# Row block 0's products with V's weights from float32 rows and weights, and the row norms' powers on GpSimd

## The chip, the cores and the metric

The kernel runs on one core of a Trainium2 chip. The core has five engines with instruction streams of their own, each worked off in order: TensorE (PE, matrix products; its weight loads are shown as PEld), VectorE (DVE), ScalarE (ACT), GpSimd (POOL) and SyncE (SP, which here issues the DMA transfers). They wait for one another by semaphores. The metric is the time of one execution on the device, in microseconds.

## The reference

One layer of an encoder for 1024 tokens of width 1024, all in float32:

```python
u = rms_norm(x, norm1_g[l])
proj = u @ w_in[l]
q, k, v, cb, cc, ch, ga, gb = jnp.split(proj, split_pts, axis=-1)
q = rms_norm(q.reshape(B, S, N_HEADS, HEAD_DIM), q_norm_g[l])
k = rms_norm(k.reshape(B, S, N_HEADS, HEAD_DIM), k_norm_g[l])
y_a = neighbourhood_attention(q, k, v, rpb[l]) @ w_attn_branch[l]
y_b = short_gated_conv(cb, cc, ch, conv_w[l]) @ w_conv_branch[l]
merged = jax.nn.sigmoid(ga) * y_a + jax.nn.sigmoid(gb) * y_b
x = x + merged @ w_o[l]
h = rms_norm(x, norm2_g[l]) @ w_mlp_in[l]
x = x + jnp.square(jax.nn.relu(h)) @ w_mlp_out[l]
```

`rms_norm(x, g)` multiplies each row of x by one over the root of its mean square, and each column by g. q and k are normed in the same way over the 64 numbers of each head. What matters here is the start: the norm of x, and its product with the 512 columns of `w_in` that give v.

## The kernel before

**Number format.** A float32 operand is scaled by a power of two (so that its largest value fits) and written as two float16 halves, hi and lo, with hi + lo the value. A product of two such operands takes three passes on TensorE: hi·hi, hi·lo and lo·hi (`PASSES`, line 447; `HH`, `HL`, `LH` name them, the left letter for the rows, the right one for the weights).

**Rows.** The 1024 tokens are 8 row blocks of 128. Block b is loaded to `xt[:, b]` (L366). `norm` (L430) is a generator with one step per `yield`: ScalarE squares the block and sums each row (L433); `rstd` (L402) turns the sum into one over the root, `ys`, with a root on ScalarE (L407) and five small VectorE operations around it (L406 ahead of the root; the reciprocal L409 and one correction step, L411, L102 and L415, behind it); the high half is x times that factor, by GpSimd (L437), for block 0 by ScalarE (L439); the low half is VectorE's (L441). `ln_step(b, n)` advances block b's generator by n steps; written out among the other work, these calls set the order on each engine.

The halves must be turned so that the columns of x lie on the partitions, in `UT`. For blocks 0 to 2 TensorE does this with eight 128 x 128 transposes per half (`turn_row`, L525), copied out of PSUM by ScalarE for the high half (L530) and VectorE for the low half (L532). For blocks 3 to 7 a DMA does it (`ln_turn`, L444), issued by SP.

**V's weights** come in two chunks `v0`, `v1` of 1024 x 256. Each needs its power of two first: for v0 the largest absolute value (`L594`), for v1 a sum of squares (`v1_square`, L623); a product with ones (`v_sum`, L541) brings the 128 partitions together, `v_scale` (L544 and what follows, to L547) makes the factor. `v_part` writes the high parts on ScalarE (L555) and the low parts on VectorE (L557), eight of each per chunk. The gain `norm1_g` is part of the factor of each row of the weights.

**Products.** `v_mms(b, j, ks, passes)` (L571) issues products of 256 columns for row block b and chunk j: 24 for each pair, for b from 0 to 2. `v_post` brings the sum out of PSUM as two halves of v (L579, L581). From block 3 on, `v_unit` does both chunks in 24 products of 512 columns (called through `unit`, L210). Then come 8 such units for Q and 8 for K (`tok_mms`, also L210), where `qk_vec` norms each head: ScalarE copies and squares (L736, L737), VectorE sums the squares of 8 heads (L740), `rstd` makes 8 factors a row, VectorE multiplies (L744, L747, L750), and two more operations make the halves (L754, L756).

**What else is queued there.** Chunks of weights are loaded to 5 buffers (`load_upto`, L234, on SP), in the order V, Q, K and so on; a buffer is free when its chunk's low parts are written. Q's weights are prepared by a generator, `prep`, stepped by `tick` among the products (squares L266, high parts L306, low parts L297). After V's part, `sforms` scales the row blocks of `xt` in place (L482), forms sums and differences of them on GpSimd (L486), and stores them.

**PSUM.** There are eight banks: three with tag "d", three "s", two "o". Transposes and sums use "o".

Of the kernel before, what the change touches and what calls it, by code (L numbers as in the profile page):

```python
# [18 lines left out]
D = 1024  # L19
# [33 lines left out]
def encoder_block(ctx: ExitStack, tc: tile.TileContext, x, weights, cols, gqk, rel, masks, out):  # L53
# [25 lines left out]
    sc = base.tile([128, 512], F32, name="sc")  # L79
    sci = sc.bitcast(I32)  # L80
    area = {"keep": [0, 0, 144], "prep": [144, 144, 240], "tmp": [240, 240, 512]}
# [289 lines left out]
    A.activation(sc[:, warm], sc[:, warm], AF.Sqrt)  # L371
# [16 lines left out]
    V.tensor_scalar(ident, idi, 0.0, None, op0=OP.is_equal)  # L388

# [27 lines left out]

    def pow2_half(ss, top, s, inv, more=0):
# [11 lines left out]
    def norm(xin, sq, u, y, pool):  # L430
# [4 lines left out]
        yield from rstd(ss, D, y, 9)  # L435
# [32 lines left out]
    ln = [norm(xt[:, b], sq, u16[:, b % 4], at(ys, b), b > 0) for b in range(8)]  # L468
# [52 lines left out]
    def turn_row(b, s):  # L521
# [5 lines left out]
        def copy():  # L527
            o, i = UT[:, s, :, b * 128:(b + 1) * 128], pt.rearrange("p (k t) -> p k t", k=8)
            if s == 0:
                A.activation(o, i, AF.Copy)  # L530
            else:
                V.tensor_copy(o, i)  # L532
# [42 lines left out]

    def v_post(b, j, s):
        hi, lo = (VT[:, b, w, 256 * j:256 * j + 256] for w in range(2))
        if s == 0:
            A.activation(hi, vps[b, j][:, :256], AF.Copy, scale=2.0 ** -20)  # L579
        else:  # L580
            V.scalar_tensor_tensor(lo, vps[b, j][:, :256], 2.0 ** -20, hi, op0=OP.mult, op1=OP.subtract)  # L581
# [10 lines left out]
    ln_step(0, 7)  # L592
    for k, n in (0, 4), (4, 2), (6, 2):
        V.tensor_reduce(sc[:, at(v0.rm, k, n)], v0.raw[k // 4][:, k % 4 * 256:(k % 4 + n) * 256].rearrange(  # L594
            "p (k w) -> p k w", k=n), axis=AX, op=OP.max, apply_absolute_value=True)
    turn_row(0, 0)()
# [4 lines left out]
    v_sum(v0, c)  # L601
    ln_step(1)
    v_scale(v0, 1e-30, pow2(v0.b, 14, v0.s, v0.inv, False, v0.more))
    ln_step(0)
    v_part(v0, 0, range(3))
    ln_step(1)
    v_part(v0, 0, range(3, 8))
    ln_step(1, 5)
    v_mms(0, 0, (0, 1), HH)
    turn_row(0, 1)()  # L610
    v_part(v0, 1, lower)
    v_mms(0, 0, range(2, 7), HH)
    copy = turn_row(1, 0)
    v_mms(0, 0, (7,), HH)
    copy()
    v_mms(0, 0, eight, LH)
    v_mms(0, 0, lower, HL)
    ln_step(2)
    ln_step(1)
    v_mms(1, 0, eight, HH)  # L620

    def v1_square(p):
        A.activation(v1.parts[:, 1, 1024 * p:1024 * p + 1024].bitcast(BF16), v1.raw[p], AF.Square,  # L623
                     accum_out=sc[:, at(v1.rm, p)])

    v_part(v0, 1, (4,))
# [3 lines left out]
    ln_step(3)  # L630
    v_part(v0, 1, (5,))
    ln_step(2, 5)
    turn_row(1, 1)()
    v_mms(0, 0, (4, 5), HL)
    v_mms(1, 0, range(6), HL)
    v_part(v0, 1, (6, 7))
    v_mms(1, 0, eight, LH)
    copy = turn_row(2, 0)
    V.tensor_reduce(sc[:, v1.a], sc[:, at(v1.rm, 0, 2)], axis=AX, op=OP.add)
    c = ones_col()  # L640
    V.tensor_tensor(c, sc[:, v1.a], sc[:, gm2], op=OP.mult)
    v_sum(v1, c)
    v_mms(0, 0, (6, 7), HL)
    v_mms(1, 0, (6, 7), HL)
    copy()
    v_scale(v1, 1e-36, pow2_half(v1.b, 14, v1.s, v1.inv, v1.more))
    v_part(v1, 0, lower)
    ln_step(2)
    v_mms(2, 0, eight, HH, HL)
    ln_step(3)  # L650
    v_part(v1, 0, (4, 5))
    v_part(v1, 1, (0, 1))
    copy = turn_row(2, 1)
    ln_step(3, 5)
    copy()
    v_part(v1, 0, (6, 7))
    for b in 0, 1:
        v_mms(b, 1, lower, HH, LH)
    v_mms(2, 0, eight, LH)
    v_mms(2, 1, lower, HH, LH)  # L660
# [3 lines left out]
    v_post(1, 0, 0)  # L664
    ln_step(3)
    ln_turn(u16[:, 3], 3, UT)
    push(cQ)
    ln_step(4)
    v_part(v1, 1, (4, 5))
    tick()  # L670
    ln_step(5)
    ln_step(4, 5)
    for b in range(3):
        v_mms(b, 1, upper, HH, LH)
# [6 lines left out]
    turned[0] = 5  # L681
    ln_step(5)
    tick()
    ln_step(6)
    v_post(1, 0, 1)
    v_post(2, 0, 1)
    ln_step(5, 5)
    tick()
    for ks in lower, (4, 5), (6, 7):
        for b in range(3):  # L690
            v_mms(b, 1, ks, HL)
# [4 lines left out]
    turned[0] = 6  # L696
    ln_step(7)
    for b in range(3):
        v_post(b, 1, 0)
        v_post(b, 1, 1)  # L700
    ln_step(6, 5)
    tick()
    ln_step(7)
    ln_step(6)
    ln_turn(u16[:, 2], 6, UT)
    turned[0] = 7
    ln_step(7, 5)
# [25 lines left out]
    def qk_vec(ps, inv, kind, res):  # L733
# [8 lines left out]
        yield from rstd(ss, HD, y, 12 if kind == "q" else 0)  # L742
# [1201 lines left out]
```

## Time and profile before

| | |
|---|---|
| median of 3 runs | 1207.05 us (1206.65 to 1208.08) |
| span of the profiled execution | 1205.3 us |
| TensorE busy | 1188.0 us, 99% |
| VectorE busy | 938.7 us, 78% |
| ScalarE busy | 759.8 us, 63% |
| GpSimd busy | 433.1 us, 36% |

How to read the lines below: in the timeline a line has start and duration in us, engine, line of the kernel, operation, what is written and read, shapes, and the count of merged instructions; in brackets stands for how long the engine had been idle, and what released it. Matmuls overlap, so that the pace of a group is best read from the starts of successive groups. In the table of groups the numbers behind the bar are busy time in us and mean duration in ns, then the idle time ahead of them. In the table of stages each engine has its busy time and count, and PEclk is the granted clock of TensorE. Of one line's instructions the three numbers are the shortest, median and longest in ns, and the start of the first and the last in us. Waits are: waiting engine and line, what it waited for, total us, how often, the longest.

### The profile page before, as it was taken

What the parts mean: (1) busy time and instruction counts of PE and PEld (TensorE: products, weight loads), DVE (VectorE), ACT (ScalarE), POOL (GpSimd) and SP (SyncE); (2) the same over time, 40 slices, a digit from 0 to 9 for tenths busy, and PEclk for the clock granted to TensorE, in tenths of its full rate; (3) what the DMA queues carried; (4) which work ended last, traced back from release to release, by engine and by line L of the source; (5) the groups of instructions that cost most, each with busy time, mean ns of one, the idle gap of its engine ahead of it and who ended that gap; (6) DMA issues with size and microseconds to landing.
All of it is one profiled execution on the core that took longest, in us unless ns stands there. A gap on an engine that the chain in (4) does not pass through costs nothing.

```text
span 1205.3 us, 17076 instructions
## 1 busy us (share of the span) xinstructions
PE 1188.0 (99%) x6294; PEld 573.8 (48%) x6294; DVE 938.7 (78%) x1759; ACT 759.8 (63%) x1183; POOL 433.1 (36%) x280
## 2 busy tenths in 40 slices
PE   6999999999999999999999999999999999999998
PEld 4444445555444444444467444444444444444444
DVE  7777988988368787877878655545548999999997
ACT  7766679867554545337779778678676744746440
POOL 1640011222311112001004465565567471553662
PEclk9999999999999999999999999999999999999999
DMA  7766657676542211224386545445465925334202
GB/s 264 151 213 141 140 119 130 133 146 123 103 123 65 67 56 53 70 93 187 57 155 183 182 159 192 149 139 193 145 247 201 352 97 217 129 138 194 105 35 105
DMA packets 171012, 173.36 MB, mean 144 GB/s; under 512 B 131504, under 2 KB 132016, under 8 KB 166832
## 3 DMA queue, kind: packets, MB, share of 16 engines
q1 hardware_dynamic: 170352, 168.07, 47.9%
q10 hardware_dynamic: 576, 4.19, 0.8%
q8 instruction: 49, 0.80, 0.3%
q14 instruction: 35, 0.29, 0.1%
HBM read 102.51 MB, written 37.75 MB: 116 GB/s over the span
## 4 chain that ended last, share of the span: by engine, by line
PE 73%; DVE 9%; ACT 1%; issue 1%; DMA 1%; DVEq 0%; ACTq 0%
PE ps_d L210 26%; PE ps_s L210 23%; PE ps_o L210 16%; PE ps_d L1039 6%; DVE w_s L1163 2%; PE ps_o L1016 1%; PE ps_s L959 1%; DVE sg L1279 1%; DVE P L999 1%; DMA u2T<-v 1%; DVE sz L973 1%; ACT w_s L1167 0%; DVE sc L317 0%; DVE m L1281 0%; ACT sg L1245 0%
## 5 line engine op out<-in xcount | busy, mean ns | idle before, releaser
L210 PEld LDWEIGHTS <-ops 128*128 128x128 f16 x1356 | 132.4, 98 | 157.3
L210 PEld LDWEIGHTS <-w 128*128 128x128 f16 x1368 | 132.8, 98 | 140.0 <-DMA u2T<-v 0.6
L1039 PE MATMUL ps_d<-uT,w_ws 128*128 128x512 f16 x528 | 123.7, 379 | 0.1
L210 PE MATMUL ps_d<-ops 128*128 128x512 f16 (+1 forms) x528 | 118.3, 374 | 0.0
L1765 ACT ACTIVATE ops<-hf,sc 128x2048 f16<-128x2048 f32 x26 | 52.0, 2000 | 97.9 <-PE ps_o L210 35.2
L210 PE MATMUL ps_s<-ops 128*128 128x512 f16 x492 | 112.9, 379 | 0.0
L1152 POOL TENSOR_TENSOR tsum<-raw 128x512 f32<-128x512 f32 x28 | 46.0, 1658 | 149.6 <-ACT raw L1138 141.6
L1345 POOL TENSOR_TENSOR as<-as 128x512 f32<-128x512 f32 x56 | 77.5, 1384 | 39.3 <-ACT as L1625 36.0
L210 PEld LDWEIGHTS <-w_s 128*128 128x128 f16 x588 | 56.8, 98 | 69.4 <-DVE w_s L1163 1.9
L210 PE MATMUL ps_d<-u2x,w 128*128 128x512 f16 (+1 forms) x360 | 80.0, 372 | 0.0
L210 PEld LDWEIGHTS <-uT 128*128 128x128 f16 x504 | 49.0, 98 | 59.6 <-DMA uT<-u 0.8
L1039 PEld LDWEIGHTS <-w_ws 128*128 128x128 f16 x528 | 51.2, 98 | 54.5 <-DVE cv L861 0.4
L210 PE MATMUL ps_o<-ops 128*128 128x512 f16 x336 | 77.1, 379 | 0.0
L1767 DVE SCALAR_TENSOR_TENSOR ops<-hf,sc,ops 128x2048 f16<-128x2048 f32 x26 | 74.0, 2846 | 3.7 <-ACT ops L1765 3.7
L210 PE MATMUL ps_o<-u2T,w 128*128 128x512 f16 (+1 forms) x324 | 71.7, 371 | 0.0
L1138 ACT ACTIVATE raw<-raw,sc 128x256 f32<-128x256 f32 x172 | 71.0, 493 | 0.8 <-DMA raw<-in_weights 0.7
L1152 POOL TENSOR_TENSOR gsum<-raw 128x512 f32<-128x512 f32 x14 | 19.0, 1376 | 133.0 <-issue 72.8
L1167 ACT ACTIVATE w<-raw,sc 128x512 f16<-128x512 f32 (+1 forms) x28 | 24.6, 927 | 54.1 <-DVE sc L426 54.1
L297 DVE SCALAR_TENSOR_TENSOR w_ws<-raw,sc,w_ws 128x512 f16<-128x512 f32 (+2 forms) x72 | 51.2, 763 | 4.7 <-ACT w_ws L306 4.7
L1658 DVE TENSOR_TENSOR as<-ps_d,as 128x512 f32<-128x512 f32 (+1 forms) x14 | 9.4, 672 | 55.8 <-ACT as L1677 53.4
L210 PE MATMUL ps_s<-u2T,w 128*128 128x512 f16 (+1 forms) x252 | 52.7, 359 | 0.0
L982 ACT ACTIVATE sz<-sz,sc 128x384 f32<-128x384 f32 (+1 forms) x64 | 37.2, 582 | 22.5 <-DVE sc L973 15.0
(357 smaller groups left out, 2629.5 us busy)
## 6 DMA issues: line engine op xcount, KB each, us to landing
raw<-in_weights SPq DMA_DIRECT2D x88, 512.0 KB, 5.4
hs<-as SPq DMA_DIRECT2D x16, 1792.0 KB, 8.7
hf<-hs SPq DMA_DIRECT2D x26, 1024.0 KB, 6.3
w2x<-in_weights SPq DMA_DIRECT2D x16, 512.0 KB, 8.1
raw<-in_weights SPq DMA_DIRECT2D x16, 384.0 KB, 3.5
xt<-in_x SPq DMA_DIRECT2D x8, 512.0 KB, 10.0
gs<-s ACTq DMA_DIRECT2D x4, 1024.0 KB, 4.0
x<-in_x SPq DMA_DIRECT2D x8, 512.0 KB, 9.8
```

The lines of the kernel that those rows point to most:

```text
L210: T.matmul(ps, l, r, start=a, stop=b)
L297: V.scalar_tensor_tensor(lo, self.raw[p][:, o:o + m], sc[:, c:c + 1], hi, op0=OP.mult, op1=OP.subtract)
L959: T.matmul(ps[:, :nb * 128], QD[:, p, e, w, i * 128:(i + 1) * 128], KD[:, 2 * p + e, lo * 128:(lo + nb) * 128], start=w == 0, stop=w == 1)
L982: A.activation(z, z, AF.Exp, scale=-1.0, bias=sc[:, d["mx"]], accum_out=sc[:, d["sm"]])
L1039: T.matmul(ps, l, r, start=a, stop=b)
L1138: A.activation(v, v, AF.Copy, scale=sc[:, at(g, 4 * i + k)])
L1152: G.tensor_tensor(t[:, o], a, b, op=OP.add)
L1163: V.scalar_tensor_tensor(o(1), w, sc[:, s], o(0), op0=OP.mult, op1=OP.subtract)
L1167: A.activation(o(0), w, AF.Copy, scale=sc[:, s])
L1345: sub.tensor_tensor(z[o], z[a], z[b], op=op)
L1765: A.activation(P[:, 1, 0], hf, AF.Copy, scale=sc[:, Rs])
L1767: V.scalar_tensor_tensor(P[:, 1, 1], hf, sc[:, Rs], P[:, 1, 0], op0=OP.mult, op1=OP.subtract)
```

## The change

Four things are changed.

1. **Block 0's product with V's weights.** The raw block of x is transposed as float32 by TensorE (`native_turn`: 8 transposes into two "o" banks, copied out by ScalarE and VectorE in turn, multiplied by `norm1_g`). The product runs on float32 operands, the raw weights as they were loaded (`native`: 8 products of 256 columns for each of the two chunks). The row factor `ys[0]` and the weights' power of two are applied to the sums, in `v_post`, with a factor per row (`raised`). The 48 float16 products and 16 transposes of block 0 are gone. Block 0's halves are still needed for Q, K and the rest: they are written later, the high half by GpSimd, and turned by a DMA ahead of block 7's.
2. **The row norms' powers.** `rpow` takes the place of `rstd` in `norm` and `qk_vec`: two GpSimd operations, a scaling with an addition and a power with exponent -0.5 from a constant column. The table of ScalarE that is loaded first is that of a square instead of a root. `rstd` stays for the second norm.
3. **The order** of the calls in V's part follows from this: V1's raw weights are used by block 0's products before block 1's transposes; the squares of block 3 come after V1's first four high parts, the scale of V1 behind the low half of block 2; the turned high half of block 1 is copied by VectorE.
4. The area of small columns grows from 512 to 524.

```diff
-    A.activation(sc[:, warm], sc[:, warm], AF.Sqrt)
+    A.activation(sc[:, warm], sc[:, warm], AF.Square)
+    minus_half = keep(8)
+    G.memset(sc[:, minus_half], -0.5)
...
+    def rpow(ss, n, y, top):
+
+        k = ss.stop - ss.start
+        v = tmp(k)
+        G.tensor_scalar(sc[:, v], sc[:, ss], 4.0 ** -top / n, 4.0 ** -top * EPS, op0=OP.mult, op1=OP.add)
+        G.tensor_tensor(sc[:, y], sc[:, v], sc[:, at(minus_half, 0, k)], op=OP.pow)
+        yield
...
-        yield from rstd(ss, D, y, 9)
+        yield from rpow(ss, D, y, 9)
...
-    ln = [norm(xt[:, b], sq, u16[:, b % 4], at(ys, b), b > 0) for b in range(8)]
+    ln = [norm(xt[:, b], sq, u16[:, b % 4], at(ys, b), True) for b in range(8)]
...
-            if s == 0:
+            if s == 0 and b == 2:
                 A.activation(o, i, AF.Copy)
             else:
                 V.tensor_copy(o, i)
...
     def v_post(b, j, s):
         hi, lo = (VT[:, b, w, 256 * j:256 * j + 256] for w in range(2))
+        c = 2.0 ** -20
+        if b == 0:
+            if s == 0:
+                raised[j] = tmp()
+                V.scalar_tensor_tensor(sc[:, raised[j]], sc[:, at(ys, 0)], c, sc[:, cV[j].s], op0=OP.mult, op1=OP.mult)
+            c = sc[:, raised[j]]
...
+    def native_turn():
+        pts = [bank("o") for _ in range(2)]
+        for k in range(8):
+            T.transpose(pts[k // 4][:, k % 4 * 128:k % 4 * 128 + 128], xt[:, 0, k * 128:(k + 1) * 128], identf)
+        for k in range(8):
+            i, c = pts[k // 4][:, k % 4 * 128:k % 4 * 128 + 128], sc[:, at(g1, k)]
+            if k % 2 == 0:
+                A.activation(x0T[:, k], i, AF.Copy, scale=c)
+            else:
+                V.tensor_scalar(x0T[:, k], i, c, None, op0=OP.mult)
+
+    def native(j, ks):
+        if (0, j) not in vps:
+            vps[0, j] = bank("d")
+        for k in ks:
+            T.matmul(vps[0, j][:, :256], x0T[:, k], cV[j].raw[k // 4][:, k % 4 * 256:k % 4 * 256 + 256],
+                     start=k == 0, stop=k == 7)
...
-    ln_step(0, 7)
...
+    native_turn()
+    v0_largest(0, 4)
+    ln_step(0, 2)
+    native(0, lower)
+    v0_largest(4, 2)
+    v0_largest(6, 2)
...
     v_sum(v0, c)
+    native(0, upper)
     ln_step(1)
     v_scale(v0, 1e-30, pow2(v0.b, 14, v0.s, v0.inv, False, v0.more))
...
+    v_part(v0, 0, range(8))
+    ln_step(1, 2)
+    native(1, lower)
+    copy = turn_row(1, 0)
+    native(1, upper)
     v_part(v0, 1, lower)
-    v_mms(0, 0, range(2, 7), HH)
-    copy = turn_row(1, 0)
-    v_mms(0, 0, (7,), HH)
     copy()
...
+    v_mms(2, 0, eight, HH, HL)
     v_part(v1, 0, lower)
-    ln_step(2)
-    v_mms(2, 0, eight, HH, HL)
     ln_step(3)
+    copy = turn_row(2, 1)
     v_part(v1, 0, (4, 5))
+    copy()
+    ln_step(3, 2)
+    v_part(v1, 0, (6, 7))
     v_part(v1, 1, (0, 1))
...
+    ln_step(7, 2)
+    ln_step(0)
+    ln_turn(u16[:, 0], 0, UT)
...
-        yield from rstd(ss, HD, y, 12 if kind == "q" else 0)
+        yield from rpow(ss, HD, y, 12 if kind == "q" else 0)
+        yield
+        yield
```

85 lines of the change are left out of this document (34 added, 51 removed).

## The prediction

> **What bounds the kernel now.** I read the page first (busy shares, slices), then TensorE's waits in the first 60 us, then busy time by stage, and last the timeline of the start.
>
> ```profile
> span 1205.3 us, 17076 instructions
> PE 1188.0 (99%) x6294; PEld 573.8 (48%) x6294; DVE 938.7 (78%) x1759; ACT 759.8 (63%) x1183; POOL 433.1 (36%) x280
> PE   6999999999999999999999999999999999999998
> ...
> PE ps_o L525 <- ACT u L439: 8.0, 1, 8.0
> PE ps_o L541 <- DVE ones L600: 1.6, 1, 1.6
> PE ps_d L571 <- ACT w_v L555: 1.5, 1, 1.5
> PE ps_d L571 <- ACT uT L530: 0.4, 1, 0.4
> PE ps_d L210 <- DMA uT<-u: 0.3, 1, 0.3
> ...
> 4.00:12.00 8.00, 1.20 (x9) 0.98 (x10) 5.20 (x19) 4.95 (x8) 0.00 (x0) 1.00 0.97 370
> 12.00:22.00 10.00, 9.64 (x80) 7.23 (x80) 9.00 (x25) 8.65 (x20) 2.24 (x2) 1.00 0.93 361
> 60.00:144.00 84.00, 84.00 (x392) 38.10 (x391) 70.36 (x170) 57.15 (x97) 18.00 (x9) 1.00 0.63 158
> ```
>
> TensorE sets the end: busy 1188 of 1205.3 us, and 84.00 of 84.00 in the stage of Q and K. What it waits for lies ahead of 12.2 us (8.0, 1.6 and 1.5 us). A gain can therefore come only from the moment at which TensorE starts the first whole row block, v_unit(3); behind it the order of the products is unchanged, and time lost later would be new waits. The same stretch in order of time:
>
> ```profile
> 4.37 1.06 ACT L433 ACTIVATE sq<-xt 128x1024 f32<-128x1024 f32 x1 [2.14 <-DMA xt<-in_x]
> 5.55 0.15 DVE L406 TENSOR_SCALAR sc<-sc 128x1 f32<-128x1 f32 x1 [0.65 <-ACT sq L433]
> 6.56 0.16 DVE L415 SCALAR_TENSOR_TENSOR sc<-sc 128x1 f32<-128x1 f32 x1
> 7.96 1.03 PE L525 MATMUL ps_o<-ident,u 128*128 128x128 f16 x8 [7.96 <-ACT u L439]
> 10.55 0.16 PE L541 MATMUL ps_o<-ones 128*128 128x1 bf16 x1 [1.56 <-DVE ones L600]
> 10.57 1.06 ACT L433 ACTIVATE sq<-xt 128x1024 f32<-128x1024 f32 x1 [0.52 <-DMA xt<-in_x]
> 12.21 0.77 PE L571 MATMUL ps_d<-w_v,uT 128*128 128x256 f16 x2 [1.49 <-ACT w_v L555]
> 15.98 1.95 PE L571 MATMUL ps_d<-w_v,uT 128*128 128x256 f16 x13
> 17.77 1.04 PE L571 MATMUL ps_s<-w_v,uT 128*128 128x256 f16 x8
> 18.64 0.61 PE L525 MATMUL ps_o<-ident,u 128*128 128x128 f16 x8
> 21.93 0.16 DVE L544 TENSOR_SCALAR sc<-ps_o 128x1 f32<-128x1 f32 x1 [0.27 <-PE ps_o L541]
> 23.20 1.70 ACT L555 ACTIVATE w_v<-raw,sc 128x256 f16<-128x256 f32 x4 [0.47 <-DVE sc L547]
> 28.90 2.07 SPq L444 DMA_TRANSPOSE uT<-u  x1
> uT<-u SPq DMA_TRANSPOSE x1, 4.4
> 33.85 5.34 PE L210 MATMUL ps_s<-w_v,uT 128*128 128x512 f16 x24
> 39.46 5.35 PE L210 MATMUL ps_d<-w_v,uT 128*128 128x512 f16 x24 [0.28 <-DMA uT<-u]
> 44.68 0.59 PE L210 MATMUL ps_s<-w_v,uT 128*128 128x512 f16 x2
> ```
>
> Two arrivals frame everything: row block 0 at 4.37 us, block 1 at 10.5. Row block 3 is turned by a DMA issued at 28.90 that lands 4.4 us later, at 33.3; v_unit(3) starts at 33.85. So that chain is already level with TensorE. v_unit(4) starts 5.61 us behind it, where the next takes 5.22 (39.46 to 44.68): about 0.4 us are lost to the turn of block 4.
>
> **The change, part by part.** *TensorE's work.* Removed: 48 products of 256 columns for block 0, 0.109 each (8 from 17.77 to 18.64), 5.2 us, and 16 transposes, 0.076 each (0.61 for 8), 1.2 us. Added: 8 float32 transposes and 16 float32 products. No row shows a float32 product. Below it is bounded by the float16 one, 0.109. Above: a float32 value is what this kernel writes as two float16 halves, so four half products; with each weight load in the open that is four times load and product.
>
> ```profile
> L571 PEld LDWEIGHTS <-uT x144: 95/98/151, 10.6 to 33.5; 128*128 128x128 f16 x144
> L1935 POOL MEMSET const-float32-1.0<- 128x1 f32 x1 | 0.1, 99 | 0.0
> L1781 POOL TENSOR_TENSOR raw<-raw 128x1024 f32<-128x1024 f32 x8 | 30.8, 3869 | 35.7 <-DVE ops L1776 35.7
> 25.89 1.12 POOL L437 TENSOR_SCALAR u<-xt,sc 128x1024 f16<-128x1024 f32 x1 [5.17 <-DVE sc L415]
> 16.48 1.27 DVE L441 SCALAR_TENSOR_TENSOR u<-xt,sc,u 128x1024 f16<-128x1024 f32 x1
> 19.43 0.69 DVE L532 COPY uT<-ps_o 128x1024 f16<-128x1024 f16 x1
> 24.27 0.87 DVE L557 SCALAR_TENSOR_TENSOR w_v<-raw,sc,w_v 128x256 f16<-128x256 f32 x2
> 26.32 1.36 DVE L557 SCALAR_TENSOR_TENSOR w_v<-raw,sc,w_v 128x256 f16<-128x256 f32 x2
> 59.36 5.12 DVE L297 SCALAR_TENSOR_TENSOR w_ws<-raw,sc,w_ws 128x512 f16<-128x512 f32 x3
> 60.22 5.34 PE L210 MATMUL ps_d<-w_ws,uT 128*128 128x512 f16 x24
> ```
>
> That gives 4 x (0.098 + 0.109) = 0.83. I take 0.46, four products with loads hidden as they are here (load 0.098 under a product of 0.109), and double for the first ones: the first 8 transposes took 1.03 us, those at 18.64 0.61. A float32 transpose lies between 0.076 and 4 x 0.13 = 0.52; I take 0.3, and it decides little, since the products behind it wait at 10.55 for the sum anyway.
>
> *When the rate doubles.* From 15.98 to 17.77 13 products took 1.79 us; with 0.109 and twice that as the two rates the change falls near 16.7, 4.5 us behind the first products at 12.21, though the granted clock reads 1.00 all along. For products that start at 6.8 I take 11.3. [...] No run here has float32 products ahead of it.
>
> *The start after the change.* Block 0 lands at 4.37; transposes and their copies (scaled, ACT and DVE in turn) let the first product start near 6.8. Four at 0.9 end at 10.4. Then the ones product for V's scale at 10.55 as before: it follows the largest absolute weights, which wait for the same DMA. Eight products at 0.46 (the first two at 0.9 or so) end at 14.5 to 15.3, of which I take 14.5; then come the transposes of block 1. Its float16 copy is ready earlier: 10.5 + 1.2 (square) + power + 1.12.
>
> *The power.* It takes the place of 1.2 us (5.55 to 6.72) of DVE and ACT. Not shown either; two GpSimd operations cost at least 2 x 0.099 = 0.2 us, and I bound it above by the dearest GpSimd row, 3.87 us. I take 0.75: one column is nearer the memset. Then block 1's copy is there at 13.6, ahead of TensorE.
>
> *DVE's chain up to V1's scale.* The transposed copy starts 0.8 us behind its transposes (18.64 to 19.43), at 15.3. Then copy 0.69, low half 1.27, four weight parts 4 x 0.435, copy 0.69, two small ones 0.35, low half of block 2 1.27: 6.0 us. GpSimd's copy of block 2 now falls into it; two weight parts took 1.36 beside such a copy, 0.87 without, so 0.45 more. The scale starts at 21.8; before 21.93. The 5 x 8 small norm operations taken from DVE (0.15 each, 6 us in all) are given back here: they lay in other places, while the later start of block 1's transposes and the low halves now stand in a row.
>
> *Block 3.* Scale to weight parts 1.27 (21.93 to 23.20), four parts 1.70, square 1.23, power 0.75, copy 1.12, low half 1.27: 21.8 + 7.34 = 29.1, and some 0.2 of handing over and a shared DVE: issued at 29.3. It lands 4.4 to 4.7 us later, near 33.9. TensorE has 72 products of 0.109 and 8 transposes left when ScalarE's copy of block 2, some 1.1 us behind the scale's start, is there (22.9): ready at 31.3, it waits 2.6 us. So the saved work is there, but it ends in a new wait for block 3's turn. v_unit(3) starts at 34.0 with the pass to TensorE, 0.15 later than before; block 4's turn, issued behind fewer DVE operations, then no longer costs its 0.4. Net -0.25, say -0.3 us.
>
> *Behind it.* Q's weights cap a larger gain: three low parts from 59.36 end at 64.48, and the first Q unit wants the last of them at 60.22 + 22 x 0.216 = 64.97: 0.5 us of slack. Their last raw tile is queued on SP behind block 4's turn, so they move with it. Block 0 gets a DMA turn on SP ahead of block 7's:
>
> ```profile
> L444 SPq DMA_TRANSPOSE uT<-u x5: 1843/2067/3593, 28.9 to 47.0; - x5
> ...
> DMA to landing us min/median/max: 4.2/5.2/6.0
> ```
>
> At worst block 7's turn moves from 47.0 to 50.6 and lands 5.2 later, at 55.8, 0.9 behind v_unit(7), which starts near 54.9. But what it waited for at 47.0 was its low half on DVE, which loses the norm operations ahead of it; issued by 48 it lands by 53.2, so I cost it at nothing, with 0.9 us at stake if DVE gains nothing. In Q and K DVE loses 5 small operations a unit, ACT one; TensorE does not wait there, so that is worth nothing. A power of 8 columns must fit a round: DVE's multiply stands behind it, and behind that the sum of the next unit (0.69 each); with 5.18 us a unit, it is harmless up to about 3.5 us.
>
> The sum is -0.3 against the profiled 1205.3 us; the runs' median is 1207.05, 1.75 above that span, and I add the difference to it: 1206.8.
>
> **The rivals.**
> A, slower: *the float32 products cost more.* At 0.83, and 1.35 for the first four, these end at 12.2 (1.6 late), and eight more add 8 x 0.37 = 3.0: block 1's transposes, and all behind them, come 4.6 us later: +4.3, 1211.4. From about 0.68 on it is a loss of more than 0.2%. For it speaks that two halves need two sets of weights; against it that loads are hidden everywhere here. [...]
>
> B, slower: *the power is dear.* At 3.87 block 1's copy comes at 16.7, 2.2 behind TensorE, and block 3's chain is another 3.1 longer: +5.0, 1212.1. It decides from about 2.5 us a power.
>
> C, faster: *block 1's transposes meet no wait.* TensorE is free at 13.4, the power costs 0.3, no DVE operation is stretched: 1.1 + 0.45 + 0.5 less: -2.3, 1204.7. For it speaks that DVE is busy 9.00 of 10 us from 12 to 22 and sheds small operations; against it that block 1 lands at 10.5 whatever is done.
>
> D: *the start is not what counts* (block 0's products are early, but nothing waited for them): this is my forecast itself, no change.
>
> **How the numbers follow.** What this kernel's measurement can tell from no change is about 0.2%, 2.4 us. My forecast, with what surrounds it inside that bound: 0.48. A 0.22, B 0.13 (both slower: 0.35). C 0.17, faster. The forecast's own range is 1205 to 1209. With A up to its own price and most of B and C, 8 in 10 lie from 1204.4 to 1212.0.
>
> **What would show it.** Right: float32 products near 0.46 once fast; a wait of TensorE of 2 to 3 us for the DMA into the transposed rows just ahead of v_unit(3), which starts within 1 us of 33.85; V1's scale within 1 us of 21.93; no TensorE wait from 60 to 144. Wrong: float32 products at 0.7 or more, powers over 2 us, v_unit(3) ahead of 32, or DVE's multiply in Q and K waiting for GpSimd with TensorE behind it.

## The result and the profile after

| | before | after |
|---|---|---|
| median of the runs | 1207.57 us (1206.65 to 1208.18, 4 runs) | 1212.31 us (1211.33 to 1212.44, 4 runs) |
| ratio after to before, 95% interval | | 1.0040 (1.0027 to 1.0054) |
| span of the profiled execution | 1205.3 us | 1210.7 us |

The change makes the kernel slower by 0.4%: 5.4 us between the two profiled spans, where 0.3 us less had been forecast. From the page of the changed kernel, the line of busy times:

```profile
PE 1191.4 (98%) x6270; PEld 576.0 (48%) x6270; DVE 928.1 (77%) x1646; ACT 752.8 (62%) x1159; POOL 478.0 (39%) x330
```

TensorE still sets the end. It is busy 3.4 us longer than before (1191.4 to 1188.0), and the rest of the 5.4 us is idle time. Where the loss lies is read from the timeline of TensorE, by looking for the same products in both kernels and taking the difference of their starts. The changed kernel (start, duration, engine and line, what is done, count, and in brackets the wait ahead of it):

```profile
4.55 1.94 PE L607 MATMUL ps_o<-identf,xt 128*128 128x128 f32 x8 [4.55 <-DMA xt<-in_x]
6.28 3.62 PE L619 MATMUL ps_d<-raw,x0T 128*128 128x256 f32 x8
11.21 0.16 PE L554 MATMUL ps_o<-ones 128*128 128x1 bf16 x1 [1.31 <-DVE ones L650]
11.31 3.69 PE L619 MATMUL ps_d<-raw,x0T 128*128 128x256 f32 x16
26.42 5.01 PE L584 MATMUL ps_s<-w_v,uT 128*128 128x256 f16 x40
33.88 7.02 PE L210 MATMUL ps_s<-w_v,uT 128*128 128x512 f16 x24 [2.45 <-DVE sc L597]
40.73 5.34 PE L210 MATMUL ps_d<-w_v,uT 128*128 128x512 f16 x24
144.41 5.34 PE L210 MATMUL ps_o<-uT,w_ws 128*128 128x512 f16 x24
150.72 5.34 PE L210 MATMUL ps_o<-uT,w_ws 128*128 128x512 f16 x24 [0.97 <-ACT qs L768]
157.48 0.16 PE L201 MATMUL ps_d<-ones 128*128 128x1 bf16 x1 [1.42 <-DVE ones L272]
157.58 0.38 PE L993 MATMUL ps_s<-kD,qD 128*128 128x256 f16 x2
```

and the kernel before at the two late places (block 3 and 4 stand in the prediction, at 33.85 and 39.46):

```profile
143.15 10.52 PE L210 MATMUL ps_o<-uT,w_ws 128*128 128x512 f16 x48
153.94 0.38 PE L959 MATMUL ps_s<-kD,qD 128*128 128x256 f16 x2
```

The differences are: block 3 of V (33.88 to 33.85) nothing; block 4 (40.73 to 39.46) 1.27 us; the first convolution unit (144.41 to 143.15) 1.26; attention (157.58 to 153.94) 3.64. During attention 0.7 us come back, in the gates, from 350 to 353 us, 2.0 us are lost again, and another 0.4 us behind them. So there are three main places, and the stretch that the change rewrote, up to block 3's start, is not among them in this execution.

**First place: block 3's 24 products take 6.85 us from start to start instead of 5.2.** The table of stages of the changed kernel shows why (stretch, its length, then for each engine its busy time and instructions; the second number from the left behind POOL is the granted clock):

```profile
32.00:34.00 2.00, 0.12 (x1) 0.13 (x2) 1.87 (x4) 0.26 (x3) 1.81 (x3) 0.97 0.66 123
34.00:36.00 2.00, 2.00 (x6) 0.63 (x6) 1.59 (x2) 2.00 (x4) 0.78 (x1) 0.50 0.93 172
36.00:38.00 2.00, 2.00 (x8) 0.82 (x7) 0.17 (x2) 1.97 (x6) 1.28 (x3) 0.68 1.05 145
```

Six products in 2 us at a clock of 0.50, where 9 belong at 0.216 us each. With 0.5 as the lowest value the cut lasted 0.12 + 2 + 1.28 = 3.4 us (each term: what is missing to 1, by 2 us, by 1/0.5). It begins as TensorE's wait of 2.45 us ends. The wait itself the prediction had; the halved clock it had not. TensorE's row names VectorE's L597 as what ended the wait, but that is the factor for block 0's sums, which block 3's products do not read. The weight load of the same products names the turn:

```profile
33.87 0.13 PEld L210 LDWEIGHTS <-uT 128*128 128x128 f16 x2 [2.73 <-DMA uT<-u]
```

The turn was not late by much, though: VectorE's copy of an earlier sum out of an "s" bank (L602) ended at 33.47 us, 0.4 us before, and whether block 3's products would have had a bank sooner is not shown.

**Second place: the end of K.** In the timeline of ScalarE and VectorE in the changed kernel

```profile
149.46 0.63 ACT L788 ACTIVATE k<-qs 128x512 f16<-128x512 f32 x1 [2.97 <-DMA kD<-k]
150.00 0.67 ACT L768 ACTIVATE qs<-ps_o,sc 128x512 f32<-128x512 f32 x1
154.09 0.23 DVE L778 TENSOR_SCALAR sc<-sc 128x8 f32<-128x8 f32 x1 [2.04 <-POOL sc L428]
157.26 0.16 DVE L272 TENSOR_TENSOR ones<-sc 128x1 bf16<-128x1 f32 x1
```

the copy of block 6's k (L788) stands ahead of block 7's first scaling (L768) and waits 2.97 us; L768 frees the PSUM bank that the second convolution unit needs (0.97 us of TensorE), and block 7's later steps drain late, with L272, which the sum product needs, behind them (1.42 us). In the kernel before, the order of the two was the other one:

```profile
147.34 0.67 ACT L736 ACTIVATE qs<-ps_o,sc 128x512 f32<-128x512 f32 x1
150.47 0.63 ACT L754 ACTIVATE k<-qs 128x512 f16<-128x512 f32 x1
```

The steps of a unit are spread by `yield`: nine for K with the root up to the copy, seven with the power and its two empty steps. Fewer steps put block 6's copy ahead of block 7's scaling.

**Third place: the gates.** SP turns the stored halves with 16, 8 and 8 DMA turns before the second group of gates. In this execution the 16 took 23.88 us, where those of the kernel before took 21.98:

```profile
304.65 23.88 SPq L1144 DMA_TRANSPOSE qD<-gs  x16
```

and TensorE waited 1.0 us for the last eight, with another 0.7 us ahead of it for which the profile shows no cause.

### The profile page after: what moved, and what is told of

Its sections match the earlier page's. It is cut to its first block, busy times and chain, and to the rows that moved or that the text cites. A ratio compares the mean times of both kernels' runs of the same rounds, so it can differ in the third digit from the quotient of the medians.

```text
span 1210.7 us, 16949 instructions
## 1 busy us (share of the span) xinstructions
PE 1191.4 (98%) x6270; PEld 576.0 (48%) x6270; DVE 928.1 (77%) x1646; ACT 752.8 (62%) x1159; POOL 478.0 (39%) x330
## 4 chain that ended last, share of the span: by engine, by line
PE 47%; DVE 3%; DMA 1%; ACT 1%; issue 1%; DVEq 0%; ACTq 0%
PE ps_d L210 19%; PE ps_s L210 16%; PE ps_o L210 12%; DVE form L1379 1%; DMA u2T<-v 1%; DVE v L1427 1%; DMA u2x<-v 0%; DVE x L1562 0%; ACT u2x L1387 0%; DVE raw L1427 0%; ACT v L1422 0%; DVE t L1531 0%; DVE u2T L1534 0%; ACT L412 0%; ACT raw L1528 0%
```

## The experiments

Each kernel was timed beside the kernel before on the same chip (medians of that: 1207.2 to 1207.6 us); the runs were taken in five groups, each on a chip of its own or at another time, so times of different groups are best compared by their ratios. "Pad" below stands for two more empty steps, "early block 3" for block 3's turn issued sooner.

**e3: is it the clock?** 24 products that nobody reads fill the wait ahead of block 3.

```diff
+    filler = bank("o")
+    for i in range(24):
+        T.matmul(filler[:, :256], UT[:, 0, i % 8, 128:256], vhome[0][:, 0, 0, i % 8 * 256:i % 8 * 256 + 256],
+                 start=i == 0, stop=i == 23)
```

> Changed kernel with 24 products of 256 columns, whose sum nothing reads, ahead of v_unit(3), in the time in which TensorE waits for the turned rows of block 3. Theory 'clock': the wait of 2.45 us lets the granted clock fall to about half for some 4 us; with the products it stays 1.00, v_unit(3) takes 5.2 instead of 6.85 us, v_unit(4) starts near 39.2, total 1.5 us less, 1210.8. Rival 'data': v_unit(3) is slow because the turned rows of blocks 3 and 4 and Q's weights arrive beside it: it still takes 6.5 us or more, total unchanged, 1212.3.

Measured: 1211.51 us, ratio 1.0034 (1.0021 to 1.0046). Timeline of TensorE:

```profile
32.01 2.78 PE L725 MATMUL ps_o<-w_v,uT 128*128 128x256 f16 x24
34.63 5.34 PE L210 MATMUL ps_s<-w_v,uT 128*128 128x512 f16 x24
39.81 5.34 PE L210 MATMUL ps_d<-w_v,uT 128*128 128x512 f16 x24
```

Block 3 starts 0.75 us later than in the changed kernel, takes 5.18 us instead of 6.85 at a granted clock of 1.00, and block 4 starts 0.9 us sooner. More work for TensorE, less time for this stretch: the slow products are the clock's doing, not their data's. K's end still loses (1.66 and 1.41 us of waits), hence the total, whose interval overlaps that of the changed kernel (1.0027 to 1.0054): the cure is read from the stretch, not from the total.

**e1 and e2: is K's end the order or the power's length?** In e1 the power stays and two empty steps are added, so that the unit has nine steps again; in e2 the root comes back in Q and K.

```diff
 e1
         yield from rpow(ss, HD, y, 12 if kind == "q" else 0)
         yield
         yield
+        yield
+        yield
 e2
-        yield from rpow(ss, HD, y, 12 if kind == "q" else 0)
-        yield
-        yield
+        yield from rstd(ss, HD, y, 12 if kind == "q" else 0)
```

> Changed kernel, but the norm of a Q or K head group takes as many generator steps as before (two more empty steps behind the power), so that the instructions of Q, K and what follows stand in the old order on each engine; the power itself stays on GpSimd. Theory 'order': the 2.4 us lost at the end of K and the 2.0 us lost in the gate units come from the shorter generator, which moves ScalarE's copy of K's block 6 ahead of the PSUM read of block 7, and later the transposes of the sums: both go, the first attention product starts near 155.2 instead of 157.6, total 1207.9. Rival 'duration': a power of 8 columns on GpSimd (2.2 us with its scaling) keeps VectorE waiting whatever the order: the end of K still loses 1.5 us or more, total 1210 to 1212.3.

> Changed kernel with the old root on ScalarE and VectorE in the norms of Q and K; the power on GpSimd stays in the row norms, and block 0 stays in float32. Both theories: the losses behind 144 us go, total near 1207.9, with 1.27 us left that arise at v_unit(3). If it is faster than the kernel with the empty steps by more than 0.5 us, the power's duration counts as well as the order. If the losses stay, neither theory holds and they come from the first part.

Measured: e1 1208.79 us, 1.0018 (1.0008 to 1.0027); e2 1210.15 us, 1.0026 (1.0015 to 1.0036). Timeline of TensorE in e1:

```profile
145.24 10.52 PE L210 MATMUL ps_o<-uT,w_ws 128*128 128x512 f16 x48
155.63 0.38 PE L995 MATMUL ps_s<-kD,qD 128*128 128x256 f16 x2
```

Both convolution units run as one group, and neither wait is left, with the same powers of the same length; in e2 the units are closed up too. It is the order. Both kernels lost 1.9 to 2.1 us at the start, though (first Q products at 62.31 and 62.16 us instead of 60.22), and e2 another 1.7 us in the gates, so their totals do not show the cure.

**e7: the edit of Q and K alone**, in the kernel before.

```diff
-        yield from rstd(ss, HD, y, 12 if kind == "q" else 0)
+        yield from rpow(ss, HD, y, 12 if kind == "q" else 0)
+        yield
+        yield
```

> The kernel before with the change's edit in Q's and K's norm alone: the power on GpSimd and two empty steps, seven steps in place of nine; V's start and the eight rows' norms untouched. Theory 'order': the edit alone makes the k copy of block 6 stand ahead of block 7's first scaling on ScalarE; the second convolution unit waits 1 to 2 us for ScalarE, the sum product before attention about 1.4 us for VectorE, attention starts near 156.3 (2.4 us after 153.9), and the time is 1.5 to 3 us over the kernel before (ratio 1.0012 to 1.0025). Rival 'worth nothing' (the prediction's price for this edit: TensorE waits nowhere between 60 and 144 us): attention starts within 0.4 us of 153.9 and the time is within 0.1% of the kernel before.

Measured: 1211.45 us, 1.0033 (1.0020 to 1.0045). The timeline of ScalarE and TensorE:

```profile
150.07 0.63 ACT L766 ACTIVATE k<-qs 128x512 f16<-128x512 f32 x1 [3.00 <-DMA kD<-k]
150.60 0.67 ACT L746 ACTIVATE qs<-ps_o,sc 128x512 f32<-128x512 f32 x1
151.32 5.34 PE L210 MATMUL ps_o<-uT,w_ws 128*128 128x512 f16 x24 [2.64 <-ACT qs L746]
158.18 0.38 PE L971 MATMUL ps_s<-kD,qD 128*128 128x256 f16 x2
```

The same order and the same two waits, here 2.64 and 1.41 us. Attention starts 4.24 us late, more than the 2.4 expected, and the time is 4.2 us up where 3 was the most expected: the copy at 150.07 us comes 0.6 later than in the changed kernel, though Q began 1.9 us sooner (59.57); what holds it there was not followed up. The edit that had been costed at nothing costs by itself nearly what the whole change does, 4.2 of 4.7 us between the medians.

**e8: both cures in the changed kernel**, e3's products and e1's steps.

> The changed kernel with both single cures: 24 products that nobody reads ahead of block 3's (as in e3_filler) and the two empty steps (as in e1_pad). Leaves nothing of the output out. Theory 'two causes': the clock stays 1.00, block 3's products take 5.2 us from about 34.5 us, Q's first products within 0.5 us of the 60.2 of the kernel before, no wait over 0.3 us before attention, which starts within 0.6 us of 153.9; the time is within 0.1% of the kernel before. Rival 'something else' (the loss does not add up from these two): the time stays over 0.15% above the kernel before, with waits elsewhere.

Measured: 1207.59 us, 1.0004 (0.9995 to 1.0013). Attention starts at 153.97 us against 153.94 in the kernel before; no wait over 0.3 us stands between block 3 and attention. The loss up to attention is made up of these two, and the gates lose nothing in this execution. What TensorE gains by its earlier start is here filled with products that nobody reads, so that nothing is won either. Three of the eleven executions took 1209.3 us at a mean clock of 0.998 or 0.999; none of them was profiled.

**e4, e5, e6: is there a gain behind block 3's turn?** In e4 block 3's square, power, halves and turn are issued sooner, and one copy out of PSUM moves ahead of block 4's low half. e5 adds the pad, e6 the root in Q and K instead of it.

```diff
     copy = turn_row(2, 0)
     v_sum(v1, c)
+    ln_step(3)
     copy()
     ln_step(2)
+    ln_step(3, 2)
     v_scale(v1, 1e-36, pow2_half(v1.b, 14, v1.s, v1.inv, v1.more))
     v_mms(2, 0, eight, HH, HL)
     v_part(v1, 0, lower)
     ln_step(3)
+    ln_turn(u16[:, 3], 3, UT)
     copy = turn_row(2, 1)
     v_part(v1, 0, (4, 5))
     copy()
-    ln_step(3, 2)
...
-    ln_step(3)
-    ln_turn(u16[:, 3], 3, UT)
...
+    v_post(1, 0, 1)
     ln_step(4)
...
-    v_post(1, 0, 1)
```

> Changed kernel with block 3's square, power and halves ahead of V1's scaled weights (ScalarE is idle for 2 us there), its turn issued some 5 us earlier, and one read of PSUM ahead of block 4's low half. Theory: V's part ends when block 3's turn lands; with it early, v_unit(3) starts at 31.5 to 32 at full clock, and v_unit(4) to v_unit(7) follow within 1 us of the pace; Q's first unit starts 3 to 4 us earlier than in the changed kernel (57.5 to 58.5), unless Q's low parts hold it, which ended about 4 us behind its start: then 58.5 to 60. Total 1208 to 1210. Rival: VectorE's queue, not the turn, holds v_unit(3) (the profile names VectorE): it starts at 33 or later, total 1211.5 or more.

> The changed kernel with block 3's square, power, halves and turn issued earlier (as in e4_early3) and with the two empty steps behind the power in Q's and K's norm (as in e1_pad). Theory 'two causes' (the start's idle gap with its slower clock, and at K's end the order on ScalarE): the shorter start of e4_early3 is kept to the end; block 3's products of V start near 30.7 us at full clock, Q's first ones near 57.2, the second convolution unit and the sum product before attention do not wait over 0.3 us, attention starts near 151.0 (about 3 us before the 153.9 of the kernel before), and the time is about 3 us under the kernel before: 1204.3 (ratio 0.9965 to 0.9985). Rival 'fixed end' (something behind attention's start, the gates' turns or the weights' loads, sets the end whatever comes before): attention starts near 151 and the time is within 1 us of the kernel before, the rest standing as a wait of TensorE between 290 and 360 us.

> As e5_early3_pad, but with the root on VectorE in Q's and K's norm in place of GpSimd's power and the empty steps (nine steps as in the kernel before). Theory 'order' (the number of steps decides, not who computes): as e5_early3_pad to within 1 us, attention starts near 151. Rival 'VectorE': root's work of 5 more operations for each of 16 norms stands in VectorE's way somewhere: Q's or K's last steps or attention late by over 1 us against e5_early3_pad.

Measured: e4 1208.20 us, 1.0007 (0.9998 to 1.0017); e5 1205.35 us, 0.9978 (0.9968 to 0.9988); e6 1205.91 us, 0.9989 (0.9981 to 0.9998). TensorE in e4:

```profile
30.68 5.34 PE L210 MATMUL ps_s<-w_v,uT 128*128 128x512 f16 x24
147.52 5.34 PE L210 MATMUL ps_o<-uT,w_ws 128*128 128x512 f16 x24 [2.05 <-ACT qs L768]
154.28 0.16 PE L201 MATMUL ps_d<-ones 128*128 128x1 bf16 x1 [1.42 <-DVE ones L272]
```

Block 3 starts 3.2 us sooner, with no wait and a full clock, and the first Q products 3.02 us sooner than in the kernel before; K's end then takes 3.47 us back. The edit moves a copy out of PSUM as well as the turn, so that it does not show how much of this either would bring alone. With the pad both units run as one group from

```profile
140.20 10.52 PE L210 MATMUL ps_o<-uT,w_ws 128*128 128x512 f16 x48
```

in e5, and attention starts at 150.58 us, 3.36 before that of the kernel before. e6 does the same (150.94): who computes the factor matters little (the intervals of e5 and e6 overlap), the number of steps does. The median gained only 1.9 us, less than the 3 expected; e13 looks for the reason.

**e10, e9 and e11: the powers in the rows' norms.** e10 puts them alone into the kernel before, in the steps where the root was. e9 is e5 with the root in the rows' norms, all of it in one step (and ScalarE's table for the root loaded first again); e11 issues the roots of rows 1 to 3 ahead of ScalarE's longer work.

```diff
 e10 (to the kernel before)
-        yield from rstd(ss, D, y, 9)
+        yield from rpow(ss, D, y, 9)
+        yield
+        yield
+        yield
+        yield
 e9 (to e5)
-        yield from rpow(ss, D, y, 9)
+        for _ in rstd(ss, D, y, 9):
+            pass
+        yield
 e11 (to e9)
+    ln_step(1, 2)
     v_part(v0, 0, range(8))
-    ln_step(1, 2)
...
+    ln_step(2, 2)
     v1_square(0)
     v1_square(1)
-    ln_step(2, 2)
...
     ln_step(3)
+    ln_step(3, 2)
     copy()
     ln_step(2)
-    ln_step(3, 2)
```

> The kernel before with the change's edit in the eight rows' norms alone: GpSimd's power in place of the root, in the same step of the row's work, followed by four empty steps; block 0 of V by three f16 passes as before, Q's and K's norm by the root. Theory 'the power alone is worth nothing' (as the prediction priced it: TensorE works without a gap from about 22 to 33.9 us in the kernel before): block 3's products within 0.7 us of 33.85, attention within 0.7 us of 153.9, time within 0.1% of the kernel before. Rival 'the power is dear' (GpSimd, busy with the rows' scaling, hands the factor on late): a wait of TensorE of 1 us or more before 34 us, time 0.1% or more above. Rival 'the power pays': block 3's products start before 33 us and the time is 0.1% or more below.

> e5_early3_pad with the eight rows' norms by the root again (five operations on VectorE and one on ScalarE for each row, issued in one step) in place of GpSimd's power. Theory 'the raw rows carry the gain' (the power in the rows' norms is worth little): VectorE gets about 0.8 to 1.2 us more work per row, of which rows 1 to 3 lie before block 3's products; TensorE's work of block 0 is as in e5_early3_pad, block 3's products start at 30.9 to 32 us, attention near 150.6 to 151.5, and the time stays 0.05% or more under the kernel before. Rival 'the power carries it' (VectorE sets the start): block 3's products start at 33 us or later, or the sum product and the scaling of V's second part come 1.5 us or more late, attention at 153 or later, and the gain of e5_early3_pad is gone.

> As e9_early3_normroot (the rows' norms by the root again), but with the roots of rows 1, 2 and 3 issued ahead of ScalarE's high halves, squares and copy, so that ScalarE's part of the root does not queue behind these. Theory 'queue' (what cost e9_early3_normroot its 17 us over e5_early3_pad is VectorE held up behind ScalarE's queue, 7.0 us in five waits there, not the root's work): VectorE waits at most 0.4 us for each root, the rest is 0.8 us of work per row; the sum product of V's second part comes 1 to 3 us after the 21.3 of e5_early3_pad, block 3's products start between 31 and 33.5 us, and the time is 1204.5 to 1208. Rival 'work' (the five operations per row are dear by themselves on an engine that is never free there): the sum product at 26 us or later, block 3's products at 36 us or later, time 1212 or more.

Measured: e10 1206.58 us, 0.9995 (0.9986 to 1.0004), block 3 at 33.23, attention 1.07 us sooner. e9 1219.26 us, 1.0101 (1.0087 to 1.0115); e11 1216.49 us, 1.0077 (1.0063 to 1.0091). In e9, where block 3 starts at 40.90, VectorE waits for ScalarE's root in the first 40 us

```profile
DVE sc L414 <- ACT sc L412: 7.0, 5, 3.4
```

that is 7.0 us in five waits, 3.4 the longest; in e11

```profile
DVE sc L414 <- ACT sc L412: 1.9, 6, 0.6
```

and still V's second scale comes at 26.66 us (21.41 in e5) and block 3 at 36.98. So for e9 the gain went with the power, as its second theory had it. For e11 neither theory is the whole of it, but "work" is the nearer one (time and block 3 beyond its marks): with most of the waits gone, 2.8 of e9's 13.9 us over e5 (by the medians; the 17 of the text above was too much) are won back. The 11.1 that are left go with the root's work on VectorE, but no run isolates it: they hold what it sets off (a wait of 4.3 us for the sum product of Q's weights at 52 us, with a clock of 0.50 from 50 to 56 us), and an earlier cut of the clock (12.39 to 15.80 us), which the profiled execution of e5 has not. In the order of the kernel before the powers are worth 0.6 us by the medians, with an interval that holds no change; in e5's order, a root issued in one step costs more than the whole gain. How much of this a root spread over more steps would save was not tried.

**e12: the changed kernel again**, for a second profile.

> The changed kernel itself, for another profiled execution. Theory 'two causes and a loose third': the start (block 3's products from about 33.9 us with a clock below 1.00, 6.5 to 7 us long, unless the wait before them is broken up by the late arrival of V's weights) and K's end (second convolution unit 0.9 to 2.1 us late, sum product before attention 1.4 us) recur, attention starts 3 to 4.5 us after 153.9; the gates' wait of 1.7 us depends on how long the 16 turns from about 304 us take (over 23 us: a wait of 1.5 us or more; under 22.5 us: none). Rival 'fixed': the gates' wait is there whatever these turns take.

Measured: 1213.58 us, 1.0052 (1.0034 to 1.0071). K's end loses as before (1.94 and 1.41 us), and the start loses in another way; attention starts 5.32 us late, past the 4.5 expected. Timeline of TensorE, and table of stages:

```profile
6.30 2.63 PE L619 MATMUL ps_d<-raw,x0T 128*128 128x256 f32 x8
11.22 0.16 PE L554 MATMUL ps_o<-ones 128*128 128x1 bf16 x1 [2.29 <-DVE ones L650]
11.32 5.31 PE L619 MATMUL ps_d<-raw,x0T 128*128 128x256 f32 x16
```

```profile
10.00:12.00 2.00, 0.78 (x3) 0.62 (x3) 1.54 (x8) 1.15 (x2) 0.24 (x2) 0.80 1.04 426
12.00:14.00 2.00, 2.00 (x6) 1.55 (x5) 1.42 (x4) 1.68 (x5) 1.64 (x2) 0.50 1.02 412
14.00:16.00 2.00, 2.00 (x9) 1.74 (x8) 1.20 (x4) 2.00 (x6) 0.00 (x0) 0.85 0.69 245
```

The first four float32 products were done 1 us sooner than in the other profile (2.63 us instead of 3.62; the first full clock is on record at 7.78 us instead of 9.98), the sum product came at the same 11.2, and so TensorE idled 2.29 us instead of 1.31. Then the clock was cut for 0.8 + 2 + 0.6 = 3.4 us, and the next 16 pairs took 5.31 us instead of 3.69. To be early by one microsecond cost 1.6. e1, e2 and e11 show the same at this place (idle times of 2.21, 2.34 and 2.44 us, pairs at 5.27 to 5.38). In the gates this execution, whose 16 turns took 22.41 us, has no wait for the turns; 1.5 us are lost later, for ScalarE (at 644.65 us).

**e13 and e14: is this the clock too?** Eight small products fill that early idle time, in e13 on top of e5, in e14 in the changed kernel.

```diff
     native(0, lower)
+    early = bank("o")
+    for i in range(8):
+        T.matmul(early[:, :128], ident, ident, start=i == 0, stop=i == 7)
```

> e5_early3_pad with eight more products of 128 columns (the identity with itself, read by nobody) behind block 0's first four float32 products, ahead of the sum product at 11.2 us. Theory 'early clock' (the executions of e5_early3_pad with a mean granted clock of 0.998 took 1205.6 to 1206.3 us, those with 1.000 took 1203.0 to 1205.1: in the former the first float32 products came early, TensorE idled over 2.2 us before the sum product, and the clock was cut at 12 to 16 us): TensorE idles under 1.8 us there in every execution, all show 0.999 or 1.000, the highest time is under 1205.3 and the median 1203 to 1204.5. Rival 'arrivals' (these executions were late because of transfers, and the clock is a bystander): the spread stays 3 us and some executions still stand above 1205.5.

> The changed kernel with the same eight small products and nothing else. Theory 'early clock': the early outcome of the changed kernel (16 load-and-product pairs in 5.3 us instead of 3.7, block 3's products at 36.3 at full clock) is gone, so every execution takes the other one: wait of 2.3 to 2.5 us before block 3's products at 33.9, clock near 0.5 behind it, Q's first products at 61.3 to 61.6, K's end as in the changed kernel; time 1211 to 1212.5. Rival 'arrivals': as the changed kernel, with one profile or the other, 1211.3 to 1214.

Measured: e13 1203.76 us (1203.41 to 1204.06, 6 runs), 0.9969 (0.9957 to 0.9980); e14 1210.51 us (1209.33 to 1211.65, 10 runs), 1.0026 (1.0016 to 1.0035). TensorE in e13:

```profile
9.84 0.95 PE L647 MATMUL ps_o<-ident 128*128 128x128 f16 x8
11.36 0.18 PE L554 MATMUL ps_o<-ones 128*128 128x1 bf16 x1 [0.57 <-DVE ones L653]
11.40 3.70 PE L619 MATMUL ps_d<-raw,x0T 128*128 128x256 f32 x16
```

The eight executions of e5 spread over 3.4 us: four with a mean clock of 1.000 took 1203.0 to 1205.1 us, four with 0.998 took 1205.6 to 1206.3. Those of e13 spread over 0.65 us, all at 0.999 or 1.000. That fits the clock as the source of the spread (no slow execution of e5 was profiled), and with the filling the two cures bring their 3 us: 3.85 us under the median of the kernel before that ran beside it (1207.61). In e14 the 16 pairs are fast again and the start loses at block 3: the wait before it comes in two parts

```profile
31.66 0.49 PE L584 MATMUL ps_s<-w_v,uT 128*128 128x256 f16 x3 [0.91 <-DVE w_v L570]
33.76 6.66 PE L210 MATMUL ps_s<-w_v,uT 128*128 128x512 f16 x24 [1.61 <-DMA uT<-u]
```

with three products between, and the clock is cut nevertheless (6.49 us from start to start). Its median lies 0.5 us under the least that was expected. Of its ten executions five have a mean clock of 0.998 and two, at 1209.33 and 1210.33 us, one of 1.000: the early idle time is filled in all of them, but the wait before block 3 does not cut the clock in every one (a cut of 3.4 us to a half in 1209 us takes the mean to 0.999 at best).

The places side by side, in us (first profile of the changed kernel, e12 its second):

| | before | changed | e12 | e8 | e13 |
|---|---|---|---|---|---|
| block 3 of V | 33.85 | 33.88 | 36.26 | 34.72 | 30.88 |
| first products of Q | 60.22 | 61.48 | 62.20 | 60.65 | 57.27 |
| attention | 153.94 | 157.58 | 159.26 | 153.97 | 150.59 |
| span | 1205.3 | 1210.7 | 1211.4 | 1205.5 | 1202.1 |

## Why the prediction was wrong

**Where it was right.** The start came out as it was worked out. From the rows of single lines in the changed kernel (shortest, median and longest in ns, first and last start in us):

```profile
L428 POOL TENSOR_TENSOR sc<-sc x24: 551/1640/2089, 9.3 to 152.4; 128x8 f32<-128x8 f32 x16, 128x1 f32<-128x1 f32 x8
L619 PEld LDWEIGHTS ps_d<-raw,x0T x32: 186/190/337, 6.1 to 16.6; 128*128 128x128 f32 x32
L619 PE MATMUL ps_d<-raw,x0T x32: 379/379/634, 6.3 to 16.9; 128*128 128x256 f32 x32
```

- *Float32 products* were priced at 0.46 us once fast; there are two pairs of load and product to each (32 for 16 products), and 16 pairs from 11.31 took some 3.5 us from start to start, 0.44 a product. The load of 190 ns, about twice that of a float16 one (98 ns), stays hidden: two pairs take 0.44 us. Rival A falls.
- *The power* was taken at 0.75 us for one column; in block 3's chain it took 0.60, with 0.19 for the scaling ahead of it (over the eight blocks 0.55 to 1.47, and 0.19 to 1.29). Rival B falls.
- *V's second scale* at 21.8 us: 21.34. *TensorE ready* at 31.3: 31.4. *Block 3's turn* issued at 29.3: 29.34. *The wait* of 2.6 us: 2.45. *Block 3* at 34.0: 33.88. *Block 4's 0.4 us* are gone, as said (in e3, too, where block 3 runs at its full pace).
- *Some of it was luck.* The sum product came at 11.21 us, not at "10.55 as before": VectorE, which now copies half of the turned block first, works without a gap from 7.90 us up to it, so that its queue and no longer the DMA sets the moment. The first full clock, on the other hand, is on record at 9.98 us (at 7.78 in e12) and not at 11.3; the 8 pairs ahead of the sum product took 3.62 us, the 16 behind it 3.69. The two misses nearly cancel: block 1's transposes start at 14.84 us where 14.5 was taken.
- *Saved work* is not the right name: 16 products of 0.44 us and 8 transposes of 0.22 us, 8.8 us, stand in place of the 6.4 us removed. What the change brings is that the products start at 6.28 us instead of 12.21.
- *Rival C* did not happen: block 1's transposes started at 14.84 us, not 13.4, and block 3's turn held TensorE. e4, e5 and e13 reach a gain of 3 us in another way, by having that turn sooner.

**First failing step:** "ready at 31.3, it waits 2.6 us. So the saved work is there, but it ends in a new wait", and from it "Net -0.25". The wait was priced at its length, as if the products behind it ran as before. They ran at half the clock for 3.4 us: block 4 came 1.27 us later instead of 0.3 sooner. e3 shows it by filling the wait. In other executions the same loss falls on the float32 products behind the sum product (e12), a place where the prediction, which let four of them end at 10.4, saw only 0.2 us of idle time; in e13 and e14, where it is filled, the 16 pairs behind it run at full pace.

**Second failing step:** "TensorE does not wait there, so that is worth nothing", of Q's and K's norm. It was read from the stage of 60 to 144 us, in which TensorE was busy 84.00 of 84.00 us; but the last unit of K drains behind 144 us, up to attention at 154 (158 in the changed kernel), outside that row. And the edit was weighed as a duration (a power harmless up to 3.5 us), while what it changed was the number of steps, and so the order on ScalarE. It cost 2.4 us here and 4.24 by itself (e7); nine steps cure it with the power (e1, e5) and with the root (e6).

**What stays open.** The 2.0 us in the gates. They were there in the first profile, perhaps in e2 and e6 (1.7 and 0.9 us at this place, without a cause in the profile), and not in e12, so that they are no fixed price of the change; the 16 turns took between 21.98 and 23.88 us in these and the kernel before, and e8 with 23.12 has no such wait. What makes them late in one execution and not in another was not settled. The prediction said nothing of the gates.

## What to carry to other kernels

Price a wait of TensorE together with the rate of the products behind it: here filling an idle time with products that nobody reads made the stretch behind it faster (block 3's products 5.18 us in e3 instead of 6.85, and the kernel by 1.6 us between the medians of e5 and e13), and in e12, where the first four products finished 1 us early, the next 16 pairs took 5.31 us instead of 3.69. Where steps of several units are interleaved by counting them, keep the count when an operation is replaced by a shorter one, and look at the unit that drains last, behind the stage that looks full. And let a saved microsecond be followed to the transfer that it ends at: the gain of this change stood behind block 3's turn, and with that issued sooner, the step count kept and the early gap filled, the kernel took 0.9969 of its former time (0.9957 to 0.9980).

## What the runs showed of the hardware

**Behind idle times of 2.21 to 2.45 us TensorE's clock was halved in five traces, behind one of 2.64 us it was not.** The granted clock went to 0.50 behind waits of 2.21, 2.29, 2.34, 2.44 and 2.45 us (e1, e12, e2, e11, changed kernel), and around waits of 4.30 and 4.31 us (e9, e11). It stayed at 1.00 around one of 2.64 us (e7, up to 151.32 us; the 24 products behind it took 5.34 us). Two waits of 0.91 and 1.61 us with three products between were followed by a cut in e14, and by none in e1, e2 and e12. In e9 the clock was cut at 25.66 us behind waits of 0.16 and 0.99 us. So in these traces the length of one wait does not decide. The stages around these two places, e9 and then e7, cut at 3.41 us:

```profile
22.24:25.66 3.42, 1.93 (x16) 0.99 (x14) 3.33 (x8) 0.83 (x2) 1.29 (x1) 1.00 0.21 86
25.66:29.07 3.41, 2.75 (x17) 2.10 (x17) 1.69 (x5) 0.38 (x1) 0.00 (x0) 0.50 0.56 161
145.98:149.39 3.41, 2.50 (x10) 0.91 (x11) 3.38 (x8) 1.09 (x3) 0.00 (x0) 1.00 1.09 207
149.39:152.81 3.42, 1.49 (x7) 0.68 (x7) 1.70 (x3) 2.68 (x6) 0.07 (x1) 1.00 1.13 253
```

A cut lasted 3.4 us, as reckoned from the stages in three places (0.12 + 2 + 1.28, 0.8 + 2 + 0.6, and in e14 0.96 + 2 + 0.44), and twice that in e11 (49.94 to 56.76 us). In e14

```profile
32.00:34.00 2.00, 0.39 (x3) 0.13 (x2) 2.00 (x5) 0.00 (x0) 1.90 (x2) 0.76 0.62 115
36.00:38.00 2.00, 2.00 (x10) 0.86 (x9) 0.40 (x1) 1.97 (x5) 0.96 (x3) 0.89 1.09 164
```

it begins near 33.0 us, 0.7 before the wait ends, so that not all of it falls on products.

The records of the clock in the traces say more. In the changed kernel the first full clock stands at 9.98 us, the cut begins 23.893 us later, at 33.87, and lasts 3.413 us; 23.893 is 7 times that. In e11 the two cuts begin 37.55 us apart (12.39 and 49.94), 11 times 3.413. So in these two traces the changes lie whole multiples of 3.41 us apart. TensorE's busy time in the 3.41 us ahead of a cut does not sort the cases: 0.84 us in the changed kernel, 1.57 in e14 and 1.93 in e9, while behind 1.49 us in e7 (149.39 to 152.81) there was no cut.

**A power of eight columns took 1.64 to 2.09 us on GpSimd** in the changed kernel, one of one column 0.55 to 1.47. **The same program has two starts:** whether the rate rises among the first four float32 products or behind them differs between executions (2.63 us for their 8 pairs in e12, 3.62 in the first profile of the changed kernel; the first full clock is on record at 7.78 and at 9.98 us).
